# A 4 KB result stored by two queues in place of one, with a handshake before the last wait

## The chip, the cores and the metric

The kernel runs on one core of a Trainium2 chip. The metric is the device time of one execution in microseconds, of the slowest (here the only) core; smaller is better. Three runs of the kernel before gave 84.14, 84.15 and 84.2 us, with a median of 84.15 us. The profile is of one further execution, which took 84.31 us and whose span, from the first to the last instruction of the kernel, was 83.0 us. Everything that concerns the change happens in the last two microseconds of that span.

## The reference

```python
batch, dim = 1024, 4096          # x and y: float32 [1024, 4096], 16.8 MB each
def reference(x, y, axis):       # axis = -1
    return np.sum(np.abs(x - y), axis=axis).astype(np.float32)
```

Some 33.6 MB are read, and 1024 sums in float32, 4 KB, are written.

## The kernel before

The 1024 rows are laid on 128 partitions, eight rows (K = 8) to each. Each partition therefore ends with eight sums, the row of the tile `ro`, which lie side by side in the output. VectorE subtracts, and ScalarE takes the absolute value and sums along the row. The eighth row is cut into five pieces that shrink towards the end (1728, 1024, 640, 384, 320 columns), so that little is left to compute when the last bytes arrive. The last piece and the final sum are VectorE's alone. `put` places each instruction in the stream of its engine, in the order written; an engine's waits stand in that same stream.

```python
PIECES = [1728, 1024, 640, 384, 320]
...
orr = out.rearrange("(p k) -> p k", p=P, k=K)        # P = 128, K = 8
ro = sbuf("ro_sums", [P, K])
s_end = nc.alloc_semaphore("s_end")
s_out = nc.alloc_semaphore("s_out")
...
# the only load that ScalarE's queue issues, ahead of the kernel's body:
put(lambda: nc.scalar.dma_start(out=yb, in_=yr[:, 0:H, :]).then_inc(s_first, 16), before="UnconditionalBranch")
...
# the eighth row, piece by piece (i-th piece, w columns)
        if i < n_part:
            sub(tx, ty, [(s_piece[i], 32)])                       # VectorE
            absum(tx, last[:, i:i + 1], s_end, absd[:, c])        # ScalarE, adds 1 to s_end
        else:
            put(lambda: nc.vector.wait_ge(s_piece[i], 32))
            put(lambda: nc.vector.tensor_sub(out=last[:, n_part:n_part + w], in0=tx, in1=ty).then_inc(s_end, 1))
            put(lambda: nc.vector.wait_ge(s_end, n_part + 2))
            put(lambda: nc.vector.reduce_sum(out=ro[:, K - 1:K], in_=last, axis=AX, apply_absolute_value=True).then_inc(s_end, 1))
...
# VectorE sets its semaphores back to zero for the next execution
take_back([(s, 32) for s in s_piece] + [(s_act, done56), (s_sub, count[0])])
done = n_part + 3
put(lambda: nc.sync.wait_ge(s_end, done))
put(lambda: nc.sync.dma_start(out=orr, in_=ro).then_inc(s_out, 16))
put(lambda: nc.sync.wait_ge(s_end, done).then_inc(s_end, -done))      # back to zero
put(lambda: nc.sync.wait_ge(s_out, 16).then_inc(s_out, -16))          # the store has landed
```

Of the kernel before, what the change touches and what calls it, by code (L numbers as in the profile page):

```python
# [18 lines left out]
class Entry:  # L19
# [26 lines left out]
    def put(self, emit, before=None):  # L46

        nc = self.nc
        hook = nc.inst_callbacks[-1]
        lower = nc._always_lower_symbolic_ap  # L50
        nc.remove_inst_callback(hook)
        nc._always_lower_symbolic_ap = False
        n = len(nc.cur_bb.bb.instructions)
        try:
            emit()
        finally:
            nc._always_lower_symbolic_ap = lower
            nc.push_inst_callback(hook)
        here = nc.cur_bb.bb.instructions
        main = nc.main_func.blocks[0].instructions  # L60
        while len(here) > n:
            mine = here.pop(n)
            if before is None:
                self.rest.append(mine)
            else:
                first = next(i for i, x in enumerate(main) if x.engine == mine.engine and x.opcode == before)
                main.insert(first, mine)
# [3 lines left out]
def kernel(ctx, tc, x, y, axis, out):  # L71
    nc = tc.nc
    P = nc.NUM_PARTITIONS
# [4 lines left out]
    orr = out.rearrange("(p k) -> p k", p=P, k=K)  # L78
# [5 lines left out]
    put = entry.put  # L84


    def sbuf(name, shape):
        return nc.alloc_sbuf_tensor(name, shape, F32, align_bytes=256).ap()
# [5 lines left out]
    ro = sbuf("ro_sums", [P, K])  # L94
# [12 lines left out]
    s_act = nc.alloc_semaphore("s_act")  # L107
    s_end = nc.alloc_semaphore("s_end")
    s_out = nc.alloc_semaphore("s_out")


    for r in (slice(0, 1), slice(1, H)):
# [24 lines left out]
    def take_back(waits):  # L137
        for s, v in waits:
            put(lambda: nc.vector.wait_ge(s, v).then_inc(s, -v))
# [39 lines left out]


    take_back([(s, 32) for s in s_piece] + [(s_act, done56), (s_sub, count[0])])
    done = n_part + 3
    put(lambda: nc.sync.wait_ge(s_end, done))
    put(lambda: nc.sync.dma_start(out=orr, in_=ro).then_inc(s_out, 16))
    put(lambda: nc.sync.wait_ge(s_end, done).then_inc(s_end, -done))
    put(lambda: nc.sync.wait_ge(s_out, 16).then_inc(s_out, -16))


# [33 lines left out]
```

## Time and profile before

| what | value |
|---|---|
| median of three runs | 84.15 us |
| span of the profiled execution | 83.0 us |
| bytes read, mean rate over the span | 33.55 MB, 404 GB/s |
| VectorE busy | 36.4 us (44% of the span) |
| ScalarE busy | 31.6 us (38%) |
| last ScalarE record (the read of an accumulator) starts | 80.63 us |

In the profile, DVE is VectorE, ACT is ScalarE and SP is SyncE; SPq and ACTq are the queues through which SyncE and ScalarE issue transfers. A line such as L184 is the line of the kernel. A row of the timeline begins with the start and the length in microseconds. A row of a transfer on SPq gives how long the engine took to issue it, not how long the bytes took. The time "to landing" runs from the start of the issue to the last increment of the transfer's semaphore. Waits and increments of semaphores are not counted as busy.

### The profile page before, as it was taken

The page shows a single profiled execution, that of the slowest core. Times are in us where ns is not written, and L with a number is a line of the kernel's source. Part 1 is how long each engine was busy: PE and PEld are TensorE (multiplying, and loading weights), DVE is VectorE, ACT ScalarE, POOL GpSimd, SP SyncE. Part 2 cuts the span into 40 slices and gives each one's busy share as a digit, 9 for nine tenths or more (in the row PEclk, how much of TensorE's full clock was granted, in tenths as well). Part 3 has the DMA queues.
Part 4 walks back from the last instruction along what each step waited for, and adds up shares of the span by engine and source line. Part 5 has one row for each costly group of instructions (what it writes and reads, how often), then busy time and mean ns, then how long its engine had stood idle before and what let it go on. Part 6 is the DMA issues. An engine that isn't in the chain of part 4 may idle for free.

```text
span 83.0 us, 115 instructions
## 1 busy us (share of the span) xinstructions
DVE 36.4 (44%) x16; ACT 31.6 (38%) x27; POOL 0.2 (0%) x4
## 2 busy tenths in 40 slices
DVE  0000000000000000000199999999279898999772
ACT  0600000000000000000000979889790599999990
POOL 0000000000000000000000000000000000000000
DMA  6996899979798999998888999869999989999950
GB/s 126 411 735 269 379 569 498 434 332 553 332 521 363 490 395 403 498 403 379 379 379 379 450 663 403 379 253 395 474 395 419 466 379 419 423 411 409 405 207 2
DMA packets 2592, 33.56 MB, mean 404 GB/s; under 512 B 416, under 2 KB 928, under 8 KB 1696
## 3 DMA queue, kind: packets, MB, share of 16 engines
q1 hardware_dynamic: 2448, 25.17, 72.3%
q10 hardware_dynamic: 144, 8.39, 23.4%
HBM read 33.55 MB, written 0.00 MB: 404 GB/s over the span
## 4 chain that ended last, share of the span: by engine, by line
DMA 63%; DVE 17%; SPq 11%; issue 6%
DMA yb_rows<-in_y_dram 63%; DVE xa_rows L134 16%; SPq L122 6%; SPq L125 4%; DVE last_piece L175 1%; DVE ro_sums L177 1%
## 5 line engine op out<-in xcount | busy, mean ns | idle before, releaser
L134 DVE TENSOR_TENSOR xa_rows<-xa_rows,yb_rows 128x4096 f32<-128x4096 f32 x4 | 17.4, 4422 | 41.1 <-DMA yb_rows<-in_y_dram 41.1
L143 ACT ACTIVATE xa_rows<-xa_rows 128x4096 f32<-128x4096 f32 x4 | 14.5, 3616 | 43.8 <-DVE xa_rows L134 43.8
L134 DVE TENSOR_TENSOR xb_rows<-xb_rows,yb_rows 128x2048 f32<-128x2048 f32 (+5 forms) x9 | 17.9, 2016 | 3.6 <-DMA yb_rows<-in_y_dram 3.5
L143 ACT ACTIVATE xb_rows<-xb_rows 128x2048 f32<-128x2048 f32 (+1 forms) x5 | 11.2, 2245 | 3.0 <-DVE xb_rows L134 3.0
L143 ACT ACTIVATE abs_piece<-xb_rows 128x1728 f32<-128x1728 f32 (+3 forms) x4 | 3.8, 944 | 0.0
L143 ACT ACT_TABLE_LOAD x1 | 1.3, 1283 | 2.4 <-PEq L217 2.4
L143 ACT ACTIVATION_READ_ACCUMULATOR xb_rows<-xb_rows 128x1 f32 x5 | 0.9, 187 | 0.0
L143 ACT ACTIVATION_READ_ACCUMULATOR xa_rows<-xa_rows 128x1 f32 x4 | 0.7, 186 | 0.0
L143 ACT ACTIVATION_READ_ACCUMULATOR abs_piece<-xb_rows 128x1 f32 x4 | 0.7, 186 | 0.0
L175 DVE TENSOR_TENSOR last_piece<-xb_rows,yb_rows 128x320 f32<-128x320 f32 x1 | 0.5, 493 | 0.3 <-DMA yb_rows<-in_y_dram 0.3
L177 DVE TENSOR_REDUCE ro_sums<-last_piece 128x1 f32<-128x324 f32 x1 | 0.5, 491 | 0.0
L169 DVE TENSOR_REDUCE ro_sums<-half_sums 128x2 f32<-128x4 f32 x1 | 0.1, 150 | 0.0
L203 POOL MEMSET const-bfloat16-1.0<- 128x1 bf16 x1 | 0.1, 101 | 0.0
L203 POOL MEMSET const-uint8-127<- 128x1 uint8 x1 | 0.1, 101 | 0.0
L203 POOL MEMSET const-float32-0.0<- 128x1 f32 x1 | 0.1, 98 | 0.2 <-issue 0.2
L203 POOL MEMSET const-float32-1.0<- 128x1 f32 x1 | 0.1, 98 | 0.0
## 6 DMA issues: line engine op xcount, KB each, us to landing
xa_rows<-in_x_dram SPq DMA_DIRECT2D x1, 6144.0 KB, 36.9
xb_rows<-in_x_dram SPq DMA_DIRECT2D x1, 6144.0 KB, 53.3
yb_rows<-in_y_dram SPq DMA_DIRECT2D x3, 2048.0 KB, 15.5
xa_rows<-in_x_dram SPq DMA_DIRECT2D x1, 2048.0 KB, 17.0
xb_rows<-in_x_dram SPq DMA_DIRECT2D x1, 864.0 KB, 17.8
yb_rows<-in_y_dram SPq DMA_DIRECT2D x1, 864.0 KB, 15.9
xb_rows<-in_x_dram SPq DMA_DIRECT2D x1, 512.0 KB, 16.7
yb_rows<-in_y_dram SPq DMA_DIRECT2D x1, 512.0 KB, 17.5
```

The costliest lines, as they stand in the source:

```text
L122: put(lambda: nc.sync.dma_start(out=xb[:, H - 1, c], in_=xr[:, K - 1, c]).then_inc(s_piece[i], 16))
L125: put(lambda: nc.sync.dma_start(out=yb[:, H - 1, c], in_=yr[:, K - 1, c]).then_inc(s_piece[i], 16))
L134: put(lambda: nc.vector.tensor_sub(out=tx, in0=tx, in1=ty).then_inc(s_sub, 1))
L143: put(lambda: nc.scalar.activation(tx if out is None else out, tx, ABS, accum_out=to).then_inc(sem, 1))
L169: put(lambda: nc.vector.reduce_sum(out=ro[:, K - 3:K - 1], in_=half, axis=AX).then_inc(s_end, 1))
L175: put(lambda: nc.vector.tensor_sub(out=last[:, n_part:n_part + w], in0=tx, in1=ty).then_inc(s_end, 1))
L177: put(lambda: nc.vector.reduce_sum(out=ro[:, K - 1:K], in_=last, axis=AX, apply_absolute_value=True).then_inc(s_end, 1))
L203: nc = _bacc.Bacc("TRN2", target_bir_lowering=False, num_devices=1)
```

## The change

The store of `ro` is cut in two by partitions: 0 to 63 go out through SyncE's queue as before, 64 to 127 through ScalarE's. The intent is that two engines hand out half a store each at the same moment, so that each has fewer rows to describe.

Both engines wait for the same count of `s_end`, and both stores add 16 to `s_out`, so that the last wait asks for 32. SyncE sets `s_end` back to zero at the end; it may do so only after ScalarE has passed its own wait for it. Hence the new semaphore `s_ack`: ScalarE adds 1 to it after its store is issued, and SyncE waits for that before it takes `s_end` back.

```diff
     s_out = nc.alloc_semaphore("s_out")
+    s_ack = nc.alloc_semaphore("s_ack")
...
     done = n_part + 3
-    put(lambda: nc.sync.wait_ge(s_end, done))
-    put(lambda: nc.sync.dma_start(out=orr, in_=ro).then_inc(s_out, 16))
+    for eng, p in ((nc.sync, slice(0, P // 2)), (nc.scalar, slice(P // 2, P))):
+        put(lambda: eng.wait_ge(s_end, done))
+        put(lambda: eng.dma_start(out=orr[p, :], in_=ro[p, :]).then_inc(s_out, 16))
+    put(lambda: nc.scalar.sem_inc(s_ack, 1))
+    put(lambda: nc.sync.wait_ge(s_ack, 1).then_inc(s_ack, -1))
     put(lambda: nc.sync.wait_ge(s_end, done).then_inc(s_end, -done))
-    put(lambda: nc.sync.wait_ge(s_out, 16).then_inc(s_out, -16))
+    put(lambda: nc.sync.wait_ge(s_out, 32).then_inc(s_out, -32))
```

## The prediction

> **What bounds the kernel now.** I read the page first for the bound of the whole, then the chain of waits for its end, then the timeline, SyncE's waits and the 0.5 us windows for the tail, because that is the only stretch that the change touches.
>
> The page says that the kernel is bound by its loads:
>
> ```profile
> DMA  6996899979798999998888999869999989999950
> DMA packets 2592, 33.56 MB, mean 404 GB/s; under 512 B 416, under 2 KB 928, under 8 KB 1696
> DMA 63%; DVE 17%; SPq 11%; issue 6%
> ```
>
> The DMA row is filled to its last slice but one. All loads are issued before the first store exists, and no instruction ahead of the last reduction changes, so nothing up to 81.46 us can move. The last pieces of the chain and of the timeline show the tail:
>
> ```profile
> 67.72 12.70 DMA yb_rows<-in_y_dram
> 80.42 0.02 issue
> 80.45 0.50 DVE last_piece L175
> 80.95 0.02 issue
> 80.97 0.49 DVE ro_sums L177
> ```
>
> ```profile
> 80.22 0.47 ACT L143 ACTIVATE abs_piece<-xb_rows 128x384 f32<-128x384 f32 x1
> ...
> 80.63 0.19 ACT L143 ACTIVATION_READ_ACCUMULATOR abs_piece<-xb_rows 128x1 f32 x1
> 80.97 0.49 DVE L177 TENSOR_REDUCE ro_sums<-last_piece 128x1 f32<-128x324 f32 x1
> 81.49 0.35 SPq L184 DMA_DIRECT2D out_dram<-ro_sums  x1
> ```
>
> The chain ends at the reduction, as it does not follow the store; the span does, up to 83.0. The reader is to see two things: ScalarE is free from 80.63 + 0.19 = 80.82 us, well before the sums are ready at 80.97 + 0.49 = 81.46, so it can issue at the same moment as SyncE; and 83.0 - 81.46 = 1.5 us of the span are the store. How the 1.5 us divide:
>
> ```profile
> SPq L186 <- SPq L186: 1.1, 1, 1.1
> ```
>
> ```profile
> out_dram<-ro_sums SPq DMA_DIRECT2D x1, 4.0 KB, 1.4
> ```
>
> ```profile
> 81.50:82.00 0.50, 0.00 (x0) 0.00 (x0) 0.00 (x0) 1.00 0.00 0
> 82.00:82.50 0.50, 0.00 (x0) 0.00 (x0) 0.00 (x0) 1.00 0.15 8
> 82.50:83.00 0.50, 0.00 (x0) 0.00 (x0) 0.00 (x0) 1.00 0.01 0
> ```
>
> In a row of windows the last but one number is the DMA share. The engine spends 0.35 us issuing and 1.1 us in the last wait (L186), and only 0.15 x 0.5 us = 0.08 us of each DMA engine's time goes into moving bytes. The records of single packets and semaphore increments in the same trace give the steps: issue 81.49 to 81.84; first packet 82.335; the 128 packets of 32 bytes over by 82.53, beside 16 four-byte packets that start at 82.38 to 82.53 (the increments on their way); the 16 increments of the store's semaphore recorded at 82.740 to 82.940, evenly 13.3 ns apart; L186 released at 82.957. So: 0.03 us to notice the sums, 0.35 us issue, 0.50 us until bytes move, 0.20 us of packets, and 0.41 us more until the last increment.
>
> **What the Trainium skill says.** "DMA: Bandwidth & Descriptors", section Rules for kernel authors, says of two transfers to disjoint partition halves "Don't bother — they serialize", since both halves spread over the same 16 engines. The trace agrees as far as it can: the undivided store already runs on 16 engines (16 increments). Its section Anatomy of one DMA — SWDGE (gpsimd) path, which is on another kind of issue, says that most of a transfer's fixed cost, about 2 us, is the receipt for the write, and none of it scales with size; the trace has 1.45 us from issue to landing, with 0.20 us of packets in it, which agrees in kind. Its section Why a DMA increments its semaphore by 16 and not by 1 says that each engine taking part posts its own increment; so two stores post 32. "Perfetto Trace Analysis", section DMA Instruction — HWDGE, says that the block that makes the descriptors is locked for one issuer at a time, and that the wait for the lock counts as part of the issue. No two issues of the two queues overlap in the trace before, so it neither confirms nor denies this: ScalarE's only one lies between two of SyncE's.
>
> ```profile
> 0.00 0.85 SPq L113 DMA_DIRECT2D xa_rows<-in_x_dram  x2
> 1.26 0.36 ACTq L114 DMA_DIRECT2D yb_rows<-in_y_dram  x1
> 2.37 0.33 SPq L115 DMA_DIRECT2D xb_rows<-in_x_dram  x1
> ```
>
> **The change part by part.**
>
> *SyncE's issue, 64 rows in place of 128.* Uncontended issues of very different transfers cost alike: 0.36 us for 8 MB on ScalarE's queue, 0.33 us for 6 MB on SyncE's (128 rows each), 0.35 us for this 4 KB. Bytes don't matter; whether rows do, no row shows, as all have 128. I take off a little: -0.03 us, with -0.15 us at most.
>
> *The gap from issue to bytes, 0.50 us, and the receipt, 82.38 to 82.74 = 0.36 us.* Neither has work in it that depends on the number of rows. Zero.
>
> *The packets.* 128 data packets as before, and 32 increments in place of 16. Each engine has 8 + 2 in place of 8 + 1, at about 9 ns each in their records: +0.01 us if both stores come together.
>
> *The increments.* They left at uneven intervals (0 to 26 ns) and arrived evenly at 13.3 ns. I read that as a pace at which this semaphore takes increments. Then 16 more cost 16 x 13.3 = +0.21 us, provided that both halves arrive together. That is the largest sure-looking term, and it rests on one semaphore's records.
>
> *ScalarE's issue.* It starts beside SyncE's, at about 81.49 us. If the descriptor block is locked, the second of the two starts up to 0.35 us later, and so do its packets and increments. The second group of 16 then arrives behind the first, which took 0.20 us, so the two delays don't add: the end moves by the greater of about 0.21 us and the lock's wait. With the whole issue under the lock, +0.35 us; with half of it, about +0.21 us.
>
> *Handshake.* ScalarE adds to s_ack after its issue, at 81.84 us or, behind a lock, 82.19. SyncE then passes two short waits (17 ns for the one in the record before). The stores land at 82.94 at the earliest of these cases, so at least 0.7 us of slack remain: zero.
>
> Sum: -0.03 + 0 + 0.01 + 0.21 = +0.19 us if the two issue side by side, and -0.03 + 0.01 + 0.35 = +0.33 us if they queue for the whole issue. Against these stands the case that the even spacing is no limit: -0.02 us. Weighted 0.45, 0.3 and 0.25 (the 0.25 stands for the first two rivals below together), that is 0.09 + 0.10 - 0.005 = +0.18 us. On the median of 84.15 us: 84.33 us.
>
> **The rivals.**
>
> *Halves are quicker.* If the issue or the 0.50 us gap grows with rows, each half saves perhaps half of the 0.35 us, at most 0.17 us, and the time would be about 84.0 us. For it: descriptors must be made for each row. Against it: the similar cost of all uncontended issues, and the +0.21 us of increments, which would eat it.
>
> *Nothing moves.* Packets are 0.08 us per engine, the remainder is latency that both halves bear side by side. Then 84.15 us, within a few hundredths. Against it: the even 13.3 ns, and the lock.
>
> *The issues queue up.* The added wait becomes a second issue on the path: 84.5 us. For it: the skill's lock. Against it: no overlap to see.
>
> *ScalarE's queue starts late.* Its load, issued at 1.26 us, has its first packet at 4.78 us, 3.5 us later, while the first packet of SyncE's queue is 1.0 us after its issue. But the 16 engines were then busy with SyncE's packets, and at 82 us they are idle. If half of it were the queue's own, the time would be about 86 us. I give this 1 in 100.
>
> **Range and chances.** All outcomes but the last lie between 84.0 and 84.5 us. The three runs before differ by 0.06 us, which widens the range a little: 84.05 to 84.6 us, for 8 in 10. Two per cent is 1.7 us; the whole store takes 1.5 us, so no version of it can be faster by that much, and slower by as much only in the last rival. Faster by over 2% 0.005, within 2% 0.98, slower by over 2% 0.015.
>
> **What would show it.** In the profile after: SyncE's issue of 64 rows at 0.30 to 0.35 us would show the first step right, 0.2 us or less would show it wrong. ScalarE's issue starting with SyncE's and lasting 0.36 us would show no lock; 0.6 us or more, a lock. 32 increments 13.3 ns apart, over some 0.42 us, would show the pace; two interleaved rows of 16 in 0.2 us would show that it was none. The wait for s_ack must end well before the wait for s_out; if it ends last, the handshake step is wrong. The prediction as a whole is wrong if anything before 81.46 us moves, or if the last landing comes earlier than before.

## The result and the profile after

The changed kernel takes 84.70 us (median of six runs, 84.66 to 84.99) against 84.15 us before (84.0 to 84.2). The ratio is 1.0076, with a 95% interval of 1.006 to 1.0091: slower by 0.55 us in the medians, and outside the predicted 84.05 to 84.6 us. As a share that is 0.8%, and so within the 2% that the prediction gave 98 chances in 100.

The page of the kernel after shows the loads unchanged:

```profile
DMA packets 2608, 33.56 MB, mean 403 GB/s; under 512 B 432, under 2 KB 944, under 8 KB 1712
DMA 63%; DVE 17%; SPq 10%; issue 6%
```

There are 16 packets more than before, which are the 16 further increments. The timeline of the kernel after, in its last rows:

```profile
80.46 0.19 ACT L144 ACTIVATION_READ_ACCUMULATOR abs_piece<-xb_rows 128x1 f32 x1
80.80 0.49 DVE L178 TENSOR_REDUCE ro_sums<-last_piece 128x1 f32<-128x324 f32 x1
81.32 0.53 SPq L187 DMA_DIRECT2D out_dram<-ro_sums  x1
81.33 0.55 ACTq L187 DMA_DIRECT2D out_dram<-ro_sums  x1
```

The loads happened to end 0.17 us sooner in this execution than in the one profiled before (the last reduction starts at 80.80 in place of 80.97 us). So the tail must be measured from the end of the reduction, not from the start of the span. The two issues do start together, 5 ns apart by their records. But each takes over half as long again as the undivided store's 0.35 us, for half the rows. The transfers and the waits of SyncE in the kernel after (the last number of a transfer is the time to landing; of a wait, the longest):

```profile
out_dram<-ro_sums SPq DMA_DIRECT2D x1, 2.0 KB, 1.7
out_dram<-ro_sums ACTq DMA_DIRECT2D x1, 2.0 KB, 2.0
```

```profile
SPq L191 <- SPq L191: 1.3, 1, 1.3
```

Both halves land later than the whole did (1.4 us). L191 is the wait for both stores; the wait for `s_ack` is too short to be listed. Windows of 0.1 us of the kernel after:

```profile
82.50:82.60 0.10, 0.00 (x0) 0.00 (x0) 0.00 (x0) 1.00 0.27 15
82.60:82.70 0.10, 0.00 (x0) 0.00 (x0) 0.00 (x0) 1.00 0.10 5
82.70:82.80 0.10, 0.00 (x0) 0.00 (x0) 0.00 (x0) 1.00 0.08 6
82.80:82.90 0.10, 0.00 (x0) 0.00 (x0) 0.00 (x0) 1.00 0.26 13
82.90:83.00 0.10, 0.00 (x0) 0.00 (x0) 0.00 (x0) 1.00 0.05 2
```

The share of the DMA engines, last but one in a row, rises twice. The two halves don't move together: they are two bursts some 0.3 us apart. The records of packets and increments give the sizes in us: the length of the issue, then the times of the first packet and of the last increment, counted from the end of the last reduction. All such times below are counted from there.

| | issue | first packet | last increment |
|---|---|---|---|
| before, 128 rows, SyncE | 0.348 | 0.871 | 1.476 |
| after, 64 rows, SyncE | 0.526 | 1.199 | 1.753 |
| after, 64 rows, ScalarE | 0.547 | 1.475 | 2.033 |

The whole is 2.033 - 1.476 = +0.557 us, as is the difference of the medians. It divides into 1.199 - 0.871 = +0.328 us until SyncE's first packet (0.178 of it in the issue, 0.150 in the gap after it), 1.475 - 1.199 = +0.276 us from there to ScalarE's first packet, and, from there to the last increment, 0.558 us in place of 0.605: -0.047 us.

### The profile page after: what moved, and what is told of

It is laid out like the page before. It is cut to its first block, busy times and chain, and to the rows that moved or that the text cites. A ratio compares the mean times of both kernels' runs of the same rounds, so it can differ in the third digit from the quotient of the medians.

```text
span 83.4 us, 118 instructions
## 1 busy us (share of the span) xinstructions
DVE 36.4 (44%) x16; ACT 31.6 (38%) x27; POOL 0.2 (0%) x4
## 4 chain that ended last, share of the span: by engine, by line
DMA 63%; DVE 17%; SPq 10%; issue 6%
DMA yb_rows<-in_y_dram 63%; DVE xa_rows L135 16%; SPq L123 6%; SPq L126 4%; DVE last_piece L176 1%; DVE ro_sums L178 1%
```

## The experiments

The +0.328 us looked at first as if two issues at once stretched each other. For the +0.276 us two readings were open: ScalarE's queue is slow, or the second of two waits for the first. Each time below is a median, set against that of the kernel before as taken alongside it; the ratio, with its 95% interval, is estimated from the single runs and can differ a little from the quotient of the two medians. Stores of part of `ro` leave the remainder of the output unwritten, which is said at each.

### e1: one half alone

```diff
-    put(lambda: nc.sync.dma_start(out=orr, in_=ro).then_inc(s_out, 16))
+    put(lambda: nc.sync.dma_start(out=orr[0:P // 2, :], in_=ro[0:P // 2, :]).then_inc(s_out, 16))
```

> SyncE alone stores partitions 0 to 63; the other half of the output is left out. If the issue and the gap to the first packet grow with rows (each half saves something by itself), the issue takes 0.17 to 0.25 us in place of 0.35, the first packet comes well before 0.84 us after the start of the issue, and the time falls by 0.1 to 0.3 us. If a store costs the same for 64 rows as for 128, the issue stays at 0.33 to 0.36 us, the landing at 1.35 to 1.45 us, and the time is within 0.1 us of before; then the 0.53 us issue of the split store is all due to its neighbour.

84.45 us against 84.18 (ratio 1.0034, 1.0023 to 1.0045). Neither case of the expectation had it: half of the work, with no neighbour, is slower than the whole. Its timeline and its time to landing:

```profile
81.69 0.53 SPq L184 DMA_DIRECT2D out_dram<-ro_sums  x1
```

```profile
L184 SPq DMA_DIRECT2D out_dram<-ro_sums x1: 531/531/531, 81.7 to 81.7; - x1
DMA to landing us min/median/max: 1.7/1.7/1.7
```

Its first packet comes 1.202 us after the reduction and its last increment after 1.756 us, within 3 ns of SyncE's half in the change. So in the change ScalarE's half does not delay SyncE's, and the +0.328 us belong to the store of 64 rows.

### e2: the whole store on ScalarE's queue

The store moves to ScalarE; SyncE waits for `s_ack` before it takes `s_end` back.

```diff
-    put(lambda: nc.sync.wait_ge(s_end, done))
-    put(lambda: nc.sync.dma_start(out=orr, in_=ro).then_inc(s_out, 16))
+    put(lambda: nc.scalar.wait_ge(s_end, done))
+    put(lambda: nc.scalar.dma_start(out=orr, in_=ro).then_inc(s_out, 16))
+    put(lambda: nc.scalar.sem_inc(s_ack, 1))
+    put(lambda: nc.sync.wait_ge(s_ack, 1).then_inc(s_ack, -1))
```

> The undivided store goes out through ScalarE's queue, with the handshake. If ScalarE's queue is slow by itself (in the split store its first packet came 0.9 us after the end of its issue, SyncE's 0.65 us), landing is 1.7 us or more and the time about 84.5 us. If the queues are alike and only sharing costs, landing is 1.4 to 1.5 us as on SyncE, and the time is 84.1 to 84.3 us.

84.17 us against 84.18 (0.9999, 0.9986 to 1.0011). The issue takes 0.348 us, to the nanosecond that of SyncE; the first packet comes after 0.880 us, the last increment after 1.483. The queues are alike, and the handshake costs nothing that times or records show.

### e3: both halves on SyncE's queue

```diff
-    put(lambda: nc.sync.dma_start(out=orr, in_=ro).then_inc(s_out, 16))
+    for p in (slice(0, P // 2), slice(P // 2, P)):
+        put(lambda: nc.sync.dma_start(out=orr[p, :], in_=ro[p, :]).then_inc(s_out, 16))
```

(and the last wait for 32)

> Both halves from SyncE, one after the other, no handshake. If issues cost a fixed 0.35 us each and don't disturb one another when they follow, the second lands 0.35 to 0.40 us later than the undivided store did: 84.5 to 84.55 us. If overlapping issues of two queues cost something of their own, this is faster than the split over two queues (84.70 us) by 0.1 us or more. If the second of two stores always loses 0.5 us whatever the queue, it is equal to it, 84.7 us.

85.16 us against 84.18 (1.0108, 1.0092 to 1.0123); every case of the expectation was too low, the first because it supposed issues of 0.35 us. They take 0.530 and 0.587 us, and the second's last increment comes after 2.395 us. Against this, the second queue of the change is a gain: two stores of 64 rows cost 0.98 us on one queue and 0.55 us on two (by the records, 0.919 and 0.557 us at the last increment).

### e4: the two halves one after the other, on two queues

ScalarE waits for a further semaphore, `s_go`, that SyncE increments once its own issue is over. The loop of the change is written out for this; only the new lines are shown, with comments on their place.

```diff
+    put(lambda: nc.sync.sem_inc(s_go, 1))                        # after SyncE's store
+    put(lambda: nc.scalar.wait_ge(s_go, 1).then_inc(s_go, -1))   # before ScalarE's
```

> Two halves on two queues, but ScalarE starts only when SyncE's issue is over. If overlap is what stretches the issues, both go back to about 0.35 us, SyncE's half lands 1.4 us after its issue, and ScalarE's 0.4 us later, so the time is 84.5 to 84.6 us: the later start costs no more than the overlap did. If ScalarE's queue is slow by itself, its half still needs 1.7 us or more from issue to landing, and the time rises above 84.8 us.

85.35 us against 84.18 (1.0132, 1.0104 to 1.016; four runs, 85.11 to 85.65). Without any overlap the issues are as long as with it:

```profile
81.45 0.52 SPq L187 DMA_DIRECT2D out_dram<-ro_sums  x1
82.16 0.52 ACTq L191 DMA_DIRECT2D out_dram<-ro_sums  x1
```

ScalarE's first packet comes 1.173 us after the start of its issue, as SyncE's (1.165). The time lies above 84.8 us, where the expectation saw a slow queue; e2 excludes that, and the records show why it is so high: 64 rows are dear on either queue, and ScalarE's issue starts 0.71 us after SyncE's. In the change ScalarE's first packet came 1.475 - 0.032 = 1.443 us after its issue, so 0.27 us of that come of SyncE's half being issued at the same time.

### e5: the split by columns

```diff
-    for eng, p in ((nc.sync, slice(0, P // 2)), (nc.scalar, slice(P // 2, P))):
+    for eng, c in ((nc.sync, slice(0, K // 2)), (nc.scalar, slice(K // 2, K))):
         put(lambda: eng.wait_ge(s_end, done))
-        put(lambda: eng.dma_start(out=orr[p, :], in_=ro[p, :]).then_inc(s_out, 16))
+        put(lambda: eng.dma_start(out=orr[:, c], in_=ro[:, c]).then_inc(s_out, 16))
```

> The store in two by columns: 128 rows of 4 sums on each queue, both at the same moment, the handshake kept. If the long issue belongs to 64 rows (0.53 us even alone) and 128 rows are the quick case, both issues take about 0.35 us and SyncE's first packet comes 0.84 us after its issue; what is left is the queueing of the second behind the first, some 0.28 us as in the split by rows, so 84.4 to 84.5 us. If the long issue comes from a store of a part of the output, whatever its rows, issues are 0.53 us and the time is 84.7 us or more. If the queueing grows with descriptors (256 in place of 128), the second comes 0.5 us after the first and the time is about 84.7 us with issues of 0.35 us.

84.40 us against 84.15 (1.0023, 1.0003 to 1.0042). That is the number of the first reading, and its short issues, but partly by luck: it had some 0.28 us for the queueing of the second store behind the first. The timeline, and windows of 0.1 us:

```profile
81.24 0.35 SPq L187 DMA_DIRECT2D out_dram<-ro_sums  x1
81.24 0.38 ACTq L187 DMA_DIRECT2D out_dram<-ro_sums  x1
```

```profile
82.00:82.10 0.10, 0.00 (x0) 0.00 (x0) 0.00 (x0) 1.00 0.05 2
82.10:82.20 0.10, 0.00 (x0) 0.00 (x0) 0.00 (x0) 1.00 0.89 24
82.20:82.30 0.10, 0.00 (x0) 0.00 (x0) 0.00 (x0) 1.00 0.59 15
82.30:82.40 0.10, 0.00 (x0) 0.00 (x0) 0.00 (x0) 1.00 0.04 1
```

Twice the rows in all, and yet short issues and one burst: the second's first packet is only 0.054 us behind the first's. What remains is at the end, which that reading did not have: 32 increments from 1.275 to 1.688 us, 31 steps of 13.3 ns without a break. That is +0.212 us on the last increment, where the prediction had 16 x 13.3 ns = +0.21.

### e6, e7, e12, e14: other numbers of rows, alone on SyncE

The edit is that of e1 with `0:32`, `0:96`, `0:48` and `0:80`; the other rows of the output are left out.

> SyncE alone stores partitions 0 to 31; three quarters of the output are left out. If any count but 128 takes one slow way, the issue is 0.52 to 0.54 us and the first packet 1.17 us after its start, as for 64 rows: 84.4 to 84.5 us. If issuing slows down as rows per DMA engine fall (8, 4, 2), the issue is 0.6 us or more and the time 84.6 us.

> SyncE alone stores partitions 0 to 95; a quarter of the output is left out. One slow way for all counts but 128: issue 0.52 to 0.54 us, 84.4 to 84.5 us. A cost that falls as rows per engine grow: issue about 0.44 us, 84.3 us. If 96 rows were as quick as 128, issue 0.35 us and 84.15 us, and 64 would be the odd case.

> SyncE alone stores partitions 0 to 47 (3 rows to each DMA engine); the remainder of the output is left out. If 64 is the one odd count, the issue is 0.35 to 0.36 us and 84.15 us. If counts between 32 and 96 are all dear, it is 0.5 us or more and 84.4 us.

> SyncE alone stores partitions 0 to 79 (5 rows to each DMA engine); the remainder of the output is left out. If 64 is the one odd count, the issue is 0.35 to 0.36 us. If counts around 64 are dear, it is about 0.5 us.

| rows | issue | first packet | last increment | median (before), ratio with interval |
|---|---|---|---|---|
| 32 | 0.360 | 0.880 | 1.418 | 84.14 (84.15), 0.9996, 0.9977 to 1.0015 |
| 48 | 0.360 | 0.887 | 1.421 | 84.16 (84.15), 0.9997, 0.9982 to 1.0011 |
| 64 (e1) | 0.531 | 1.202 | 1.756 | 84.45 (84.18), 1.0034, 1.0023 to 1.0045 |
| 80 | 0.362 | 0.885 | 1.453 | one execution |
| 96 | 0.353 | 0.877 | 1.454 | 84.21 (84.15), 1.0001, 0.9985 to 1.0017 |
| 128 (before) | 0.348 | 0.871 | 1.476 | |

The expectations for 32 and 96 rows had a slow way of all counts but 128, or a slope. Neither is there. What holds is the last case of e7's expectation and the first of e12's and e14's: 64 is the one dear count of the six. Otherwise rows hardly count (0.06 us between 32 and 128 at the last increment).

### e11, e13: what it is about 64

e11 stores 64 rows of 4 sums, `orr[0:P // 2, 0:K // 2]`; e13 stores `orr[32:96, :]`. The remainder of the output is left out.

> SyncE alone stores 64 rows of 4 sums (16 bytes each); three quarters of the output are left out. If the count of 64 rows makes the issue long, it stays at 0.52 to 0.54 us and the time at 84.45 us. If it is 64 rows of 32 bytes in particular, it falls to 0.35 us and 84.15 us.

> SyncE alone stores partitions 32 to 95; the other half of the output is left out. If the count of 64 is what is dear, the issue is 0.52 to 0.54 us. If it is a range that begins or ends at partition 64, it is 0.35 us.

e11: 84.38 us against 84.15 (1.0032, 1.002 to 1.0045), issue 0.531 us, first packet after 1.198: half the bytes, and no difference to e1. e13, one execution, has the longest of all issues of a store:

```profile
L184 SPq DMA_DIRECT2D out_dram<-ro_sums x1: 598/598/598, 81.3 to 81.3; - x1
DMA to landing us min/median/max: 1.8/1.8/1.8
```

So it is the count of 64 rows, not the bytes, not the cut at partition 64. Why e13's issue is some 0.07 us longer than the others of 64 rows, one execution does not say.

### e9: the split with the cut at 96

```diff
-    for eng, p in ((nc.sync, slice(0, P // 2)), (nc.scalar, slice(P // 2, P))):
+    for eng, p in ((nc.sync, slice(0, 96)), (nc.scalar, slice(96, P))):
```

> The split by rows with the cut at 96 in place of 64: SyncE stores 96 rows, ScalarE 32, all else as in the change. If 64 rows are what is dear, both issues take 0.35 to 0.38 us, the second's first packet comes less than 0.1 us after the first's, and only the 16 further increments at 13.3 ns stay: about 84.35 us. If any split by rows over two queues is dear, 84.6 us or more.

84.37 us against 84.15 (1.002, 1.0011 to 1.003): this one number removes 0.33 us of the 0.55.

```profile
81.43 0.36 SPq L187 DMA_DIRECT2D out_dram<-ro_sums  x1
81.43 0.40 ACTq L187 DMA_DIRECT2D out_dram<-ro_sums  x1
```

```profile
82.20:82.30 0.10, 0.00 (x0) 0.00 (x0) 0.00 (x0) 1.00 0.04 3
82.30:82.40 0.10, 0.00 (x0) 0.00 (x0) 0.00 (x0) 1.00 0.50 27
82.40:82.50 0.10, 0.00 (x0) 0.00 (x0) 0.00 (x0) 1.00 0.28 13
```

Short issues, one burst, first packets 0.045 us apart, and 32 increments again without a break from 1.264 to 1.677 us. The second of the two issues is some 0.035 us longer than alone (0.396 us against 0.360 for 32 rows), and so in e5 (0.382 us against 0.348): that is all that two short issues add to each other's length.

### e8 and e10: another semaphore for the stores

In both, `s_out` is allocated ahead of `s_act` and `s_end` and so is semaphore 110 in place of 112 (the other two move up by one); e8 is otherwise the kernel before, e10 the split by columns.

```diff
+    s_out = nc.alloc_semaphore("s_out")
     s_act = nc.alloc_semaphore("s_act")
     s_end = nc.alloc_semaphore("s_end")
-    s_out = nc.alloc_semaphore("s_out")
```

> The kernel before with s_out allocated ahead of s_act and s_end, so that it is semaphore 110 in place of 112; nothing else. In the trace before, increments of semaphores 104 to 108 keep at least 13.3, 11.7, 10, 8.3 and 6.7 ns between them, and those of 101 and 102 5 and 3.3, so the pace seems to depend on the number modulo 8. If the even 13.3 ns of s_out are such a pace and bind, increments of 110 come as close as 3.3 ns and the last lands up to 0.06 us earlier: 84.1 us, at the edge of what the times can show, but plain in the records. If they are a matter of the store, the spacing stays 13.3 ns.

> The split by columns with s_out allocated first of the three, as semaphore 110. If the +0.2 us of the split by columns are 16 more increments at the 13.3 ns of semaphore 112, they shrink to a few hundredths: the last landing 1.50 to 1.55 us after the last reduction in place of 1.69, and 84.15 to 84.25 us. If the second store's landing is late for another reason, it stays at 1.69 us and 84.4 us.

e8: 84.12 us against 84.15 (0.9994, 0.9975 to 1.0012), no difference that the times show. The records show one. The steps between increments, in ns, in the kernel before and in e8:

```
before 112: 13 14 13 13 14 13 13 14 13 13 14 13 13 14 13    last at 1.476 us
e8     110:  9  4 11 15  9  4  6  6  3  3 17 12 19 18 31    last at 1.441 us
```

The even 13.3 ns are gone. The steps are uneven, as those between the increments' packets are (0 to 26 ns in e8), though not one by one the same. e10: 84.30 us against 84.15 (1.0014, 1.0004 to 1.0023), last increment after 1.602 us in place of 1.688. Beside e5's 84.40 us the times alone can't tell the two apart; the records can. Both cases of the expectation missed: 0.086 of the 0.212 us went. Between the later increments of e10 four steps of 30 to 34 ns stand among steps of 3 to 14, and why isn't known. So the pace of semaphore 112 is shown; that it makes up the whole +0.2 us of a second store is not.

### e15: a load of 64 rows

The first load of the kernel before, 128 rows of 16 KB, is cut into two of 64 rows.

```diff
-    for r in (slice(0, 1), slice(1, H)):
-        put(lambda: nc.sync.dma_start(out=xa[:, r, :], in_=xr[:, r, :]).then_inc(s_first, 16), before="Drain")
+    for p, r in ((slice(0, P // 2), slice(0, 1)), (slice(P // 2, P), slice(0, 1)), (slice(0, P), slice(1, H))):
+        put(lambda: nc.sync.dma_start(out=xa[p, r, :], in_=xr[p, r, :]).then_inc(s_first, 16), before="Drain")
```

(and the waits for `s_first` for 64 in place of 48)

> The kernel before with its first load (128 rows of 16 KB, issued in 0.38 us while nothing else runs) cut into two loads of 64 rows, both on SyncE's queue. If 64 rows are dear for loads too, each of the two is issued in 0.5 us or more. If it belongs to stores, each takes 0.33 to 0.40 us. The end of the kernel is bound by the loads as a whole, so the time may rise by a few tenths in the first case and not in the second.

One execution: 90.9 us, beside 84.54 us of the kernel before, far more than either reading allowed. Line L113 issues the two loads of 64 rows and then one of 128:

```profile
L113 SPq DMA_DIRECT2D xa_rows<-in_x_dram x3: 553/578/585, 0.0 to 1.2; - x3
```

The first issue takes 0.553 us, when nothing else runs; before it was 0.377 us. So in this one execution the long issue belongs to a load too. (The third, of 128 rows, is the longest, 0.585 us in place of 0.424, but stands behind the other two.) ScalarE's load is issued 0.96 us later than before. Most of the 6 us come from elsewhere. Windows of the kernel before, then of e15 (the last number is GB/s):

```profile
2.00:4.00 2.00, 0.00 (x0) 1.28 (x1) 0.00 (x0) 1.00 0.94 401
4.00:6.00 2.00, 0.00 (x0) 0.00 (x0) 0.00 (x0) 1.00 1.44 623
6.00:8.00 2.00, 0.00 (x0) 0.00 (x0) 0.00 (x0) 1.00 0.87 377
```

```profile
2.00:4.00 2.00, 0.00 (x0) 0.66 (x1) 0.00 (x0) 1.00 1.09 238
4.00:6.00 2.00, 0.00 (x0) 0.62 (x1) 0.00 (x0) 1.00 0.84 172
6.00:8.00 2.00, 0.00 (x0) 0.00 (x0) 0.00 (x0) 1.00 1.11 246
```

Compare the first rows, 238 and 401 GB/s: from 4.78 us on, the rows of the kernel before carry packets of ScalarE's load as well. The engines are as busy and move little more than half as much: the median of the first 64 packets of 16 KB is 1282 ns in e15 and 614 ns before. For these loads of 64 partitions the bytes themselves come at about half the rate. The 4 KB store is too small to show that.

## Why the prediction was wrong

*What bounds the kernel, and that nothing ahead of the store moves:* right. The whole difference, 0.557 us, lies behind the last reduction.

*SyncE's issue, 64 rows in place of 128 (-0.03 us):* this is the step that failed, and with it the zero for the gap up to the first packet. The prediction looked at issues of very different sizes, all of 128 rows, found them alike, and took 64 rows for a little cheaper. The issue is 0.178 us longer and the gap 0.150 us (e1, alone). That is +0.328 us where the sum had -0.03, and more than the whole sum of the prediction. Its sign for this step had 0.30 to 0.35 us, or 0.2 and less; an issue of 0.526 us lies on neither side.

*ScalarE's issue (up to 0.35 us later if the descriptor block is locked):* the second half comes 0.276 us after the first, of the predicted size, but partly by luck: it isn't a lock of a whole issue. With 128, 96 or 32 rows the second comes 0.045 to 0.054 us after the first (e5, e9). So this term, too, is large only because the rows are 64. The Trainium skill's "Perfetto Trace Analysis", section DMA Instruction — HWDGE, has one lock and counts the wait for it as part of the issue; here ScalarE's issue was hardly longer than alone (0.547 us against 0.516 in e4), and of its delay of 0.27 us 0.24 lay behind the end of the issue (first packet 0.896 us after it, against 0.657 in e4).

*The increments (+0.21 us):* 16 more in the same pace were shown in e5 and e9, with +0.212 and +0.201 us at the last increment, but how much of that is the pace stays open: on semaphore 110 (e10) 0.126 us of it stayed. (The packets of the increments left 0 to 24 ns apart in the kernel before, not up to 26.) In the change itself they cost nothing: the first 16 end at 1.753 us, the second 16 begin at 1.833, and wait for no one. The prediction had said that this and the second's delay don't add.

*Packets, receipt and handshake:* right in size; from ScalarE's first packet to the last increment 0.047 us less than before. `s_ack` was passed 0.65 us after the reduction, the wait for the stores 2.05 us after it, and e2 has the handshake at no cost. One comparison went too far, though: of the 1.45 us from issue to landing only 0.41 came after the packets, so a receipt that is most of the fixed cost is not what this trace shows.

*The rivals:* that halves are quicker is refuted by e1, that ScalarE's queue starts late by e2, that nothing moves by the time itself. With issues that queue up, the prediction came to 84.5 us, for lack of the 64 rows. The range, up to 84.6 us, allowed nothing for an issue of 64 rows that is dearer than one of 128, although the prediction itself said that no row showed it.

The Trainium skill's "DMA: Bandwidth & Descriptors", section Rules for kernel authors, says of disjoint partition halves "Don't bother — they serialize". The case agrees in the verdict, 84.70 us against 84.15, and adds that a good half of the loss, 0.33 us, is not the serializing but the count of 64.

Open stays why 64 is dear: no record shows what the issuing engine or the descriptor block does in those 0.33 us. Nor do these runs tell 64 rows apart from four rows to each of 16 engines, if the rows are shared out evenly: every store here raised its semaphore by 16 single increments. Counts other than the six weren't tried. No run was faster than the kernel before beyond the noise.

## What to carry to other kernels

This store of 4 KB is nearly all latency: of 1.45 us from issue to landing its packets took 0.20. Two stores side by side cost what one costs, plus whatever the second adds at the last wait (0.13 to 0.21 us by the records where neither part had 64 rows), so splitting can gain only from a shorter issue, and no issue here was shorter for having fewer rows. Before a transfer is cut, measure one with the exact shape of the part, alone: here half a store was slower than the whole, and a load cut into two of 64 partitions ran at about half the rate. If a cut is needed, 96 and 32 rows, or halves of the columns, were cheaper than 64 and 64.

## What was not expected of the hardware

- Issuing a transfer of 64 rows took 0.52 to 0.60 us on either queue where nothing was queued ahead; stores of 32, 48, 80, 96 and 128 rows took 0.35 to 0.36 us alone. From the start of the issue to the first packet of a lone store it was 1.17 to 1.24 us with 64 rows, against 0.84 to 0.86 us with the others.
- Two loads of 64 partitions moved 172 to 246 GB/s between 2 and 8 us, where one of 128, while it ran alone (2 to 4 us), moved 401 GB/s (one execution of each).
- Increments of semaphore 112 never came closer than 13 ns, those of 110 as close as 3 ns. In the kernel before, the closest for 104 to 108 were 13, 11, 10, 8 and 6 ns, and for 101 to 103, three loads of one size, 5, 3 and 2 ns. So the closest step goes with the number of the semaphore; that it is a limit set by the number is inferred, and only 110 against 112 was tried on one store.
